# A hybrid decoder step on one core: reordered loads, a pipelined second split of x, half-width recurrence states, and convolution products on GpSimd

## Chip, cores and metric

The kernel runs on one core of a Trainium2 chip. The metric is the device time of one launch in microseconds. The core has five engines with their own instruction streams: TensorE (PE, matrix products; PEld is its weight load), VectorE (DVE), ScalarE (ACT), GpSimd (POOL) and SyncE (SP, which issues most DMAs).

## What is computed

One layer of a decoder over 1024 prompt positions and 8 x 8 sample positions (1088 columns together, width 1024), all in fp32:

```python
h = rmsnorm(x, norm_mix_pre)
(a_b, a_c, a_u, b_p, c_q, c_f, c_i, c_g, d_a, d_g) = split(h @ w_in, 10)   # 256 wide each
ya = a_b * causal_dwconv(a_c * a_u, conv_w)                  # width 3
yb = pool_scale * (W_grp @ (windowed means(b_p) - b_p))
f  = lb + (1 - lb) * sigmoid(c_f)                             # 4 heads of 64
S_t = diag(f_t) S_{t-1} + (1 - f_t) i_t^T ;  o_t = S_t^T silu(c_q)_t
yc = head_rmsnorm(o) * silu(c_g)
yd = silu(layernorm(causal_dwconv(d_a * sigmoid(d_g), conf_dw) + conf_b))   # width 31
x = x + rmsnorm(concat(ya, yb, yc, yd) @ w_out)
x = x + rmsnorm((silu(g @ w_gate) * (g @ w_up)) @ w_down),   g = rmsnorm(x)
```

The samples carry their own histories and states; all final states are outputs too.

## The kernel before

Activations lie transposed: 8 tiles of 128 features by 1088 columns (`ys[k]` holds x, then other results). Each fp32 product is three passes on TensorE: an operand is split into a rounded part and its remainder, both in a reduced format, `XH[k]` and `XL[k]` for x and two halves of a `wop` tile for the weights; the passes are hi by hi, hi by low, low by hi. A split is a copy on ACT (the rounded part) and a subtraction on DVE (the remainder).

`w_in` is taken in 20 units of 128 output columns, in the order `UNITS` (12, 10, 8, 18, 16, ...). The first four are called U0 to U3: U0 is half of the recurrence's input i, U1 of its gate f, U2 of its query q, U3 of the convolution module's gate. A unit has 8 steps, one for each k, of 9 products (three passes by the three column pieces `CH`). Weights arrive in raw tiles (`load_w`, `load_unit`, 4 buffers, one half unit each); `split_w`, `prep_half` and `prep_steps` split them. PSUM has 6 banks for units (`mm`, two units of three) and 2 for everything small (`sm`).

The start is a block written out by hand for ACT, DVE and PE:

1. For each k, raw x times the norm's gain is split into `XH`, `XL` (`split_x`), squared on ACT and added up on DVE (`acc0`), while PE multiplies U0 by it, and U1 three tiles later. So U0 to U2 work on x that has the gain but not yet the reciprocal root.
2. PE sums the squares over the partitions (line 266), DVE makes the reciprocal root `r0` in 12 short instructions, PE broadcasts it (line 189) and ACT copies it to `rb0`. U1 and U2 are multiplied by `rb0` when they leave PSUM (to `HF[0]` and `HQ[0]`, then sigmoid and silu).
3. The second split: for each k, x is scaled by gain and `rb0` (on DVE, `y<-y,prm,h` in the trace), copied to `XH[k]` (line 219) and subtracted to `XL[k]`. From U3 on, all units work on this x.

After the block, `drive` emits a unit's products and calls `hook` between them. `hook` has a budget of DVE time, counted up by the products and spent on the generators in the lists `first`, `crit` and `bulk`, in this order; each `yield` gives what the step costs, and `yield None` (`wait(n)`) says that the generator is not to be asked again in this hook. So the order of PE and DVE instructions is fixed when the program is built. The two hand-written blocks each keep their own order; the compiler's scheduler merges them, which is why the trace shows the recurrence's first DVE steps between those of the second split. `take` and `give` count buffers: `z` (two tiles), `h` (six), `sm`, `mm` and so on. `until` calls `hook` with no products between.

The generators that the change touches or its steps depend on:

- `hgrn(j)`: the recurrence for two of the four heads. Lines 700 and 702 make f and 1 - f on ACT; then DVE reciprocals and products for the first half of the columns, then products of the two heads (line 738, which wait for all of that), and so on by doubling block sizes. At the end it walks 9 groups of 128 columns: an update `up` (line 874), a transpose of k (853), the heads' outputs (878), the product with the state (890), and on DVE the new state in one of three tiles `sbd`. A state tile is 128 x 128 with two 64 x 64 blocks on its diagonal, one for each head, and zeros elsewhere.
- `d_conv(j)`: the convolution of width 31. For the samples it multiplies windows of u by the taps into a z tile (4 DVE instructions for half of the samples) and reduces it; for the prompt it does 31 DVE steps over 1024 columns. It is the main filler of `bulk`.
- `c_v`, `d_gate`, `d_val` and the other handlers take a unit out of PSUM; several need a z tile.

The mixers' outputs then go through `w_out`, and the second half of the layer runs the large feed-forward products, with Strassen-like combinations of blocks; the change does not touch it.

Of the kernel before, what the change touches and what calls it, by code (L numbers as in the profile page):

```python
# [52 lines left out]
def body(ctx, tc, xT, win, wout, wgu, wdn, par, con, msk, poolw, s_conv, s_pool, s_hgrn, s_conf,  # L53
# [31 lines left out]
    taps = T(mp, [P, 62], "taps")  # L85
    SY.dma_start(taps, par[:, NPAR:])
    cst = T(const, [P, NCON], "cst")
    SY.dma_start(cst, con)
    ident = cst[:, C_ID:C_ID + P]
# [103 lines left out]
    def load_unit(n):  # L193
        wraw[n] = [load_w(win[n][:, h * 4:h * 4 + 4]) for h in range(2)]
# [14 lines left out]

    for k in range(KT):  # L210
        if k in (0, 2):
            load_unit(U0 if k == 0 else U1)
        SY.dma_start(ys[k], xT[k * P:(k + 1) * P, :])
    load_unit(U2)

    def split_x(k, scale, parts):
# [23 lines left out]
    with tc.manual_schedule(engines={mybir.EngineType.Activation, mybir.EngineType.DVE, mybir.EngineType.PE}):  # L240
        sq, acc0 = {}, None
        pu[U0], pu[U1] = banks(), banks()
        prep_half(U0, 0)
        for k in range(KT):
            split_x(k, pc("g_mix", k), CH if k == 0 else [(0, NT)])
            if k == 0:
                prep_half(U0, 1)
            if k in (2, 3):
                prep_half(U1, k - 2)
            sq[k] = ht(NT)  # L250
            S.activation(sq[k], ys[k], AF.Square)
            mm_unit(U0, k)
            if k >= 3:
                mm_unit(U1, k - 3)
            if k == 1:
                acc0 = sq[0]
            if k >= 1:
                TT(acc0, acc0, sq[k], ALU.add)
        zv.append(zt())
        for c, (o, n) in enumerate(CH):  # L260
            S.copy(zv[0][:, o:o + n], pu[U0][c][:, :n])
        mm_unit(U1, 5)
        st = sm()
        V.memset(st[64:, 8:9], 1.0)
        for i, (go, gn) in enumerate(GRP):
            PE.matmul(st[:gn, i:i + 1], acc0[:, go:go + gn], ones[:, :1], start=True, stop=True, skip_group_check=True)
        mm_unit(U1, 6)
        for r0 in rsqrt_steps(st[:, :9], [P, 9], 1.0 / D, "x"):
            pass
        prep_half(U2, 0)  # L270
        prep_half(U2, 1)
        load_unit(U3)
        mm_unit(U1, 7)
        pu[U2] = banks()
        rb0 = ht(NT)
        for c, (o, n) in enumerate(CH):
            ps = sm()
            for i, (go, gn) in enumerate(GRP):
                if o <= go < o + n:
                    bcast(ps, r0[:, i:i + 1], gn, go - o)  # L280
            S.copy(rb0[:, o:o + n], ps[:, :n])
            mm_unit(U2, c)
        HF[0] = ht()
        for c, (o, n) in enumerate(CH):
            TT(HF[0][:, o:o + n], pu[U1][c][:, :n], rb0[:, o:o + n])
        S.activation(HF[0], HF[0], AF.Sigmoid)
        mm_unit(U2, *range(3, KT))
        prep_half(U3, 0)
        prep_half(U3, 1)
        for k in range(KT):  # L290
            STT(ys[k], ys[k], pc("g_mix", k), rb0, ALU.mult, ALU.mult)
            split_x(k, None, [(0, NT)])
            if k == 3:
                HQ[0] = ht()
                for c, (o, n) in enumerate(CH):
                    TT(HQ[0][:, o:o + n], pu[U2][c][:, :n], rb0[:, o:o + n])
                S.activation(HQ[0], HQ[0], AF.Silu)

# [119 lines left out]
    for t in qz:  # L418
        GP.memset(t, 0.0)
    sbd = [T(mp, [P, P], f"sbd{i}") for i in range(3)]  # L420
    for t in sbd:
        GP.memset(t, 0.0)

# [46 lines left out]
    def d_conv(j):  # L470
# [17 lines left out]
        for w in range(31):  # L488
# [206 lines left out]
    def hgrn(j):  # L695
# [172 lines left out]
        for g in range(9):  # L868
# [4 lines left out]
            if g < 8:  # L873
                PE.matmul(up, kt[:gn], v[:gn, g], start=True, stop=True, skip_group_check=True)
                k_token(g + 1, tp)
                pe(0.22)
# [12 lines left out]
            elif g > 0:  # L889
                PE.matmul(op[:, :gn], sbd[g % 3], q[:, go:go + gn], start=False, stop=True, skip_group_check=True)  # L890
                pe(0.22)
# [3 lines left out]
            if g < 8:  # L895
                nkt = k_evac(g + 1, tp)
                nx = sbd[(g + 1) % 3]
                for h, hs in enumerate(HEADS):
                    if g == 0:
                        V.tensor_copy(nx[hs, hs], up[hs, hs])  # L900
                    else:
                        STT(nx[hs, hs], sbd[g % 3][hs, hs], tots[128][hs, g:g + 1], up[hs, hs])
                give(sm=1)
                kt = nkt
                if g == 7:
                    for hs in HEADS:
                        SY.dma_start(o_hgrn_p[j][hs], nx[hs, hs])
                yield 0.4
            else:
# [976 lines left out]
```

## Time and profile before

| | us |
|---|---|
| median of 3 runs | 1186.87 (1184.63 to 1189.62) |
| the profiled execution | 1185.16, span 1182.8 |
| PE busy | 1145.1 (97%), granted clock 0.988 |
| PE weight loads | 1108.7 (94%) |
| DVE busy | 902.6 (76%) |
| ACT busy | 457.1 (39%) |
| POOL busy | 104.9 (9%) |

The span runs from the first to the last instruction; the 2.4 us around it belong to the launch. A timeline row reads: start, length, engine, line, operation, output from inputs by the program's names, shapes, count; in brackets the idle time ahead of it and who ended it. Several like instructions in a row are merged. A row of the chain of waits reads: start, length, engine, what. A row of the lines view reads: line, engine, operation, names, shapes and count, then busy time and mean ns, then idle time ahead of the group and who ended it. Line 65 is the helper for all `tensor_tensor`, 71 that for `scalar_tensor_tensor`.

### The profile page before, as it was taken

The numbers are of one execution on the slowest core, as the hardware profiler recorded it, in microseconds if no ns is written. First come the engines' busy times: TensorE is split into PE (matmuls) and PEld (weight loads), VectorE is DVE, ScalarE is ACT, GpSimd is POOL, SyncE is SP. The second block draws the span as 40 slices with busy tenths as digits, with TensorE's granted clock in tenths as the row PEclk, the third lists the DMA queues.
The fourth block names the chain that finished last, engine by engine and source line by source line (L and its number), as shares of the span: only waits on it lengthen the run. The fifth ranks groups of instructions, "written<-read, shape, count | busy, mean of one in ns | idle before, by whom it ended". The sixth has DMA issues, their size and how long they took to land.

```text
span 1182.8 us, 21814 instructions
## 1 busy us (share of the span) xinstructions
PE 1145.1 (97%) x8435; PEld 1108.7 (94%) x8435; DVE 902.6 (76%) x1827; ACT 457.1 (39%) x993; POOL 104.9 (9%) x170
## 2 busy tenths in 40 slices
PE   5979999999999999999999999999999999999995
PEld 4959989998899999999999999999999999999995
DVE  6498998997774678786766877787776658888666
ACT  7452431253264454343323443444444441223321
POOL 1000000000000000000000000000000232336323
PEclk9979999999999999999999999999999999999998
DMA  7101112211126114122331543553554787853555
GB/s 263 37 19 41 37 37 57 52 37 22 48 92 208 52 62 136 44 73 82 110 117 46 186 144 89 185 163 98 168 166 140 212 266 213 278 177 110 155 105 100
DMA packets 103319, 136.90 MB, mean 116 GB/s; under 512 B 25008, under 2 KB 72240, under 8 KB 103216
## 3 DMA queue, kind: packets, MB, share of 16 engines
q1 hardware_dynamic: 94864, 108.71, 29.5%
q0 software_dynamic: 8352, 26.81, 8.5%
q8 instruction: 66, 1.08, 0.4%
q14 instruction: 37, 0.30, 0.1%
HBM read 94.90 MB, written 40.57 MB: 115 GB/s over the span
## 4 chain that ended last, share of the span: by engine, by line
PE 88%; DVE 7%; ACT 2%; DMA 1%; issue 1%; SPq 0%; POOL 0%; DVEq 0%; ACTq 0%; POOLq 0%
PE p L1396 30%; PE mm L989 16%; PE p L1629 14%; PE p L1124 8%; PE p L1305 6%; PE p L1506 6%; PE mm L148 3%; PE sm L803 2%; DVE wop L65 1%; DVE y L71 1%; DVE xl L65 1%; DVE raw L65 1%; DMA raw<-wgu 1%; DMA y<-xT 1%; PE p L1090 1%
## 5 line engine op out<-in xcount | busy, mean ns | idle before, releaser
L65 DVE TENSOR_TENSOR wop<-raw,wop 128x512 fp32r<-128x512 f32 (+2 forms) x296 | 195.8, 675 | 98.1 <-ACT wop L1012 89.8
L1396 PE MATMUL p<-xh,wop 128*128 128x272 f32 x1216 | 235.6, 289 | 0.6 <-DVE c L65 0.6
L1012 ACT CAST wop<-raw 128x512 fp32r<-128x512 f32 (+1 forms) x240 | 141.9, 604 | 239.6 <-DVE raw L65 111.5
L1396 PEld LDWEIGHTS p<-xh,wop 128*128 128x128 f32 x1216 | 193.1, 188 | 0.8 <-DVE c L65 0.8
L989 PE MATMUL mm<-xh,wop 128*128 128x256 f32 (+2 forms) x816 | 172.8, 338 | 6.9 <-ACT xh L219 6.9
L1396 PE MATMUL p<-t,wop 128*128 128x272 f32 x912 | 177.2, 288 | 0.0
L1396 PE MATMUL p<-xl,wop 128*128 128x272 f32 x608 | 175.0, 288 | 0.0
L989 PEld LDWEIGHTS mm<-xh,wop 128*128 128x128 f32 x816 | 132.4, 192 | 15.1 <-ACT xh L219 9.5
L1396 PEld LDWEIGHTS p<-t,wop 128*128 128x128 f32 x912 | 144.7, 188 | 0.0
L1396 PE MATMUL p<-x,wop 128*128 128x272 f32 x456 | 130.5, 286 | 0.0
L1396 PEld LDWEIGHTS p<-xl,wop 128*128 128x128 f32 x608 | 114.6, 188 | 0.0
L1124 PE MATMUL p<-xh,wop 128*128 128x272 f32 x512 | 99.1, 290 | 0.0
L989 PE MATMUL mm<-xl,wop 128*128 128x256 f32 (+2 forms) x408 | 94.7, 341 | 1.3 <-DVE xl L65 1.0
L1396 PEld LDWEIGHTS p<-x,wop 128*128 128x128 f32 x456 | 85.8, 188 | 0.0
L1629 PE MATMUL p<-xh,wop 128*128 128x272 f32 x456 | 82.0, 288 | 0.2 <-DVE acc L65 0.2
L1629 PE MATMUL p<-xl,wop 128*128 128x272 f32 x456 | 81.4, 288 | 0.0
L1124 PEld LDWEIGHTS p<-xh,wop 128*128 128x128 f32 x512 | 81.0, 188 | 0.0
L65 DVE TENSOR_TENSOR raw<-raw,raw 128x512 f32<-128x512 f32 (+1 forms) x123 | 71.4, 591 | 9.7 <-DMA raw<-wgu 7.1
L71 DVE SCALAR_TENSOR_TENSOR y<-u,taps,y 128x1024 f32<-128x1024 f32 x60 | 77.0, 1283 | 1.5
L1124 PE MATMUL p<-xl,wop 128*128 128x272 f32 x256 | 73.9, 289 | 1.1 <-DVE xl L65 1.1
L1305 PE MATMUL p<-xh,wop 128*128 128x272 f32 x384 | 74.1, 290 | 0.0
L989 PEld LDWEIGHTS mm<-xl,wop 128*128 128x128 f32 x408 | 66.5, 192 | 7.4 <-DVE xl L65 3.9
(312 smaller groups left out, 2017.3 us busy)
## 6 DMA issues: line engine op xcount, KB each, us to landing
raw<-wgu SPq DMA_DIRECT2D x88, 256.0 KB, 3.3
hx<-hi SPq DMA_DIRECT2D x84, 136.0 KB, 2.4
raw<-win SPq DMA_DIRECT2D x40, 256.0 KB, 2.9
hx<-x SPq DMA_DIRECT2D x64, 136.0 KB, 2.7
raw<-wdn SPq DMA_DIRECT2D x32, 256.0 KB, 3.7
xh<-hx POOLq DMA_DIRECT2D x15, 544.0 KB, 5.3
xl<-hx POOLq DMA_DIRECT2D x15, 544.0 KB, 5.4
x<-hx POOLq DMA_DIRECT2D x12, 544.0 KB, 5.3
```

The costliest lines, as they stand in the source:

```text
L65: (eng or V).tensor_tensor(out, a, b, op)
L71: (eng or V).scalar_tensor_tensor(out=out, in0=a, scalar=s, in1=b, op0=op0, op1=op1)
L148: PE.matmul(ps[c][:, :n], hl[:, wi, kk], X[k][:, o:o + n], start=k == 0 and wi == 0 and X is XH, stop=k == KT - 1 and wi == 1)
L803: PE.matmul(ps[:rows, g * P:(g + 1) * P], kk[:, o:o + rows], qz[hf][:, :, g * 64:(g + 1) * 64], start=True, stop=True, skip_group_check=True)
L989: PE.matmul(ps[c][:, :w], hl[:, wi, kk], X[k][:, o:o + w], start=k == order[0] and wi == 0 and X is XH, stop=k == order[-1] and wi == 1)
L1012: S.copy(hl[:, 0], raw)
L1090: PE.matmul(st[:, i:i + 1], sq[:, a:a + P], ones[:, :1], start=first and i == 0, stop=last, skip_group_check=True)
L1124: PE.matmul(ps[nt][:, :PW], WO[nt][k // 4][:, wi, kk:kk + P], X[k][:, o:o + PW], start=k == korder[0] and wi == 0 and X is XH, stop=k == k ...
L1305: PE.matmul(ps[r][:, :PW], w[:, wi, (k % 4) * P:(k % 4 + 1) * P], X[k][:, o:o + PW], start=k == 0 and wi == 0 and X is XH, stop=k == KT - ...
L1396: PE.matmul(ps[:, :PW], wop[:, wi, kk * P:(kk + 1) * P], x(kk, xi), start=first and kk == 0 and wi == 0 and xi == 0, stop=kk == 3 and wi == 1,
L1506: PE.matmul(ps[:, :n], wd[:, wi, kk * P:(kk + 1) * P], hops[k][xi][:, o:o + n], start=first and kk == 0 and wi == 0 and xi == 0, stop=not ...
L1629: PE.matmul(ps[:, :PW], ws[name][wi][q], x[:, xi, pr], start=first and q == 0 and wi == 0 and xi == 0, stop=q == 1 and wi == 1, skip_group ...
```

## The change

Four edits:

- **Loads.** U0's and U1's halves are spread between the x tiles, x tile 0 comes in two pieces, the constants `cst` after x tile 3 and the convolution's `taps` last.
- **The start.** In step 1 a tile's square and sum come one tile later (`square(k - 1)` after the split of k), and U0's second and U1's halves are split at other places. The sums over the partitions come one step of U1 earlier, and two of U1's steps move behind them. In step 3 the subtraction for tile k - 1 comes after the scaling of tile k; `HF[0]` and `HQ[0]` leave PSUM at other places, and both sigmoid and silu come behind the last copy to `XH`.
- **States.** `sbd` is 128 x 64, one head above the other, with no zeros. Update and state product are done head by head on TensorE; the new state is one DVE instruction instead of two.
- **Sample products.** The 16 window products of `d_conv` run on GpSimd, and five waits stand ahead of the reduction.

```diff
-    SY.dma_start(taps, par[:, NPAR:])
-    SY.dma_start(cst, con)
...
-    for k in range(KT):
-        if k in (0, 2):
-            load_unit(U0 if k == 0 else U1)
-        SY.dma_start(ys[k], xT[k * P:(k + 1) * P, :])
+    load_half(U0, 0)
+    load_x(0, CH[0], (CH[1][0], NT - CH[1][0]))
+    load_x(1)
+    load_half(U0, 1)
+    load_x(2)
+    load_half(U1, 0)
+    load_x(3)
+    SY.dma_start(cst, con)
+    load_x(4)
+    load_half(U1, 1)
+    for k in range(5, KT):
+        load_x(k)
     load_unit(U2)
+    SY.dma_start(taps, par[:, NPAR:])
...
         for k in range(KT):
             split_x(k, pc("g_mix", k), CH if k == 0 else [(0, NT)])
-            if k == 0:
+            if k == 1:
                 prep_half(U0, 1)
-            if k in (2, 3):
-                prep_half(U1, k - 2)
-            sq[k] = ht(NT)
-            S.activation(sq[k], ys[k], AF.Square)
+            if k in (2, 5):
+                prep_half(U1, k // 5)
+            if k >= 1:
+                square(k - 1)
             mm_unit(U0, k)
             if k >= 3:
                 mm_unit(U1, k - 3)
-            if k == 1:
-                acc0 = sq[0]
-            if k >= 1:
-                TT(acc0, acc0, sq[k], ALU.add)
+        square(KT - 1)
...
-        mm_unit(U1, 5)
         st = sm()
...
-        mm_unit(U1, 6)
+        mm_unit(U1, 5)
...
-        mm_unit(U1, 7)
+        mm_unit(U1, 6)
...
-            mm_unit(U2, c)
-        HF[0] = ht()
...
-        S.activation(HF[0], HF[0], AF.Sigmoid)
-        mm_unit(U2, *range(3, KT))
-        prep_half(U3, 0)
-        prep_half(U3, 1)
-        for k in range(KT):
-            STT(ys[k], ys[k], pc("g_mix", k), rb0, ALU.mult, ALU.mult)
-            split_x(k, None, [(0, NT)])
-            if k == 3:
-                HQ[0] = ht()
...
+            if c == 0:
+                mm_unit(U1, 7)
+            else:
+                mm_unit(U2, c - 1)
+        mm_unit(U2, *range(2, KT))
...
+        for k in range(KT):
+            scale_x(k)
+            if k >= 1:
+                low_x(k - 1)
+            if k == 2:
+                HF[0] = evac_r(U1)
+            if k == 4:
+                prep_half(U3, 0)
+                prep_half(U3, 1)
         S.activation(HF[0], HF[0], AF.Sigmoid)
+        low_x(KT - 1)
+        HQ[0] = evac_r(U2)
+        S.activation(HQ[0], HQ[0], AF.Silu)
...
-    sbd = [T(mp, [P, P], f"sbd{i}") for i in range(3)]
-    for t in sbd:
-        GP.memset(t, 0.0)
+    sbd = [T(mp, [P, 64], f"sbd{i}") for i in range(3)]
...
-                TT(t[:, b * 8:(b + 1) * 8], win_ap, dwb[:, 0])
+                TT(t[:, b * 8:(b + 1) * 8], win_ap, dwb[:, 0], eng=GP)
+            yield from wait(5)
...
-            yield 2.6
+            yield 1.4
...
-                PE.matmul(up, kt[:gn], v[:gn, g], start=True, stop=True, skip_group_check=True)
+                for hs in HEADS:
+                    PE.matmul(up[hs, :64], kt[:gn, hs], v[:gn, g, hs], start=True, stop=True, skip_group_check=True)
...
-                PE.matmul(op[:, :gn], sbd[g % 3], q[:, go:go + gn], start=False, stop=True, skip_group_check=True)
+                for hs in HEADS:
+                    PE.matmul(op[hs, :gn], sbd[g % 3][hs], q[hs, go:go + gn], start=False, stop=True,
+                              skip_group_check=True)
...
-                for h, hs in enumerate(HEADS):
-                    if g == 0:
-                        V.tensor_copy(nx[hs, hs], up[hs, hs])
-                    else:
-                        STT(nx[hs, hs], sbd[g % 3][hs, hs], tots[128][hs, g:g + 1], up[hs, hs])
+                if g == 0:
+                    V.tensor_copy(nx, up[:, :64])
+                else:
+                    STT(nx, sbd[g % 3], tots[128][:, g:g + 1], up[:, :64])
```

In the new second split, `scale_x` is the scaling and the copy to `XH`, `low_x` the subtraction, `evac_r` the three products with `rb0` out of PSUM.

More of the change, by code (lines that the diff above doesn't have):

```diff
@@ L206, in body, with load_half, load_x @@
     U0, U1, U2, U3 = UNITS[:4]
-    for k in range(KT):
-        if k in (0, 2):
-            load_unit(U0 if k == 0 else U1)
-        SY.dma_start(ys[k], xT[k * P:(k + 1) * P, :])
+    def load_half(n, h):
+        wraw.setdefault(n, []).append(load_w(win[n][:, h * 4:h * 4 + 4]))
+    def load_x(k, *cols):
+        for o, n in cols or [(0, NT)]:
+            SY.dma_start(ys[k][:, o:o + n], xT[k * P:(k + 1) * P, o:o + n])
+    load_half(U0, 0)
[10 more added lines that the diff above has]
+        load_x(k)
     load_unit(U2)
+    SY.dma_start(taps, par[:, NPAR:])
     def split_x(k, scale, parts):
@@ L240, in body, with square @@
     with tc.manual_schedule(engines={mybir.EngineType.Activation, mybir.EngineType.DVE, mybir.EngineType.PE}):
-        sq, acc0 = {}, None
+        sq = {}
         pu[U0], pu[U1] = banks(), banks()
+        def square(k):
+            sq[k] = ht(NT)
+            S.activation(sq[k], ys[k], AF.Square)
+            if k:
+                TT(sq[0], sq[0], sq[k], ALU.add)
         prep_half(U0, 0)
@@ L265, in body @@
         for i, (go, gn) in enumerate(GRP):
-            PE.matmul(st[:gn, i:i + 1], acc0[:, go:go + gn], ones[:, :1], start=True, stop=True, skip_group_check=True)
-        mm_unit(U1, 6)
+            PE.matmul(st[:gn, i:i + 1], sq[0][:, go:go + gn], ones[:, :1], start=True, stop=True, skip_group_check=True)
+        mm_unit(U1, 5)
         for r0 in rsqrt_steps(st[:, :9], [P, 9], 1.0 / D, "x"):
@@ L281, in body, with scale_x, low_x, evac_r @@
             S.copy(rb0[:, o:o + n], ps[:, :n])
-            mm_unit(U2, c)
-        HF[0] = ht()
-        for c, (o, n) in enumerate(CH):
-            TT(HF[0][:, o:o + n], pu[U1][c][:, :n], rb0[:, o:o + n])
-        S.activation(HF[0], HF[0], AF.Sigmoid)
-        mm_unit(U2, *range(3, KT))
-        prep_half(U3, 0)
-        prep_half(U3, 1)
-        for k in range(KT):
-            STT(ys[k], ys[k], pc("g_mix", k), rb0, ALU.mult, ALU.mult)
-            split_x(k, None, [(0, NT)])
-            if k == 3:
-                HQ[0] = ht()
-                for c, (o, n) in enumerate(CH):
-                    TT(HQ[0][:, o:o + n], pu[U2][c][:, :n], rb0[:, o:o + n])
-                S.activation(HQ[0], HQ[0], AF.Silu)
+            if c == 0:
[3 more added lines that the diff above has]
+        mm_unit(U2, *range(2, KT))
+        def scale_x(k):
+            STT(ys[k], ys[k], pc("g_mix", k), rb0, ALU.mult, ALU.mult)
+            S.copy(XH[k], ys[k])
+        def low_x(k):
+            TT(XL[k], ys[k], f32(XH[k]), ALU.subtract)
+        def evac_r(n):
+            t = ht()
+            for c, (o, w) in enumerate(CH):
+                TT(t[:, o:o + w], pu[n][c][:, :w], rb0[:, o:o + w])
+            return t
+        for k in range(KT):
[7 more added lines that the diff above has]
+                prep_half(U3, 1)
+        S.activation(HF[0], HF[0], AF.Sigmoid)
+        low_x(KT - 1)
+        HQ[0] = evac_r(U2)
+        S.activation(HQ[0], HQ[0], AF.Silu)
     MM = 0.1135
@@ L905, in hgrn @@
                 if g == 7:
-                    for hs in HEADS:
-                        SY.dma_start(o_hgrn_p[j][hs], nx[hs, hs])
-                yield 0.4
+                    SY.dma_start(o_hgrn_p[j], nx)
+                yield 0.25
             else:
```

## The prediction

> **What bounds the kernel now.** I read the windows first, cut where the work changes character: the loads, the first products on raw x, the second split of x, the rest of the mixers, everything after. Columns are: stretch, length, then busy time of PE, its weight loads, DVE, ACT, POOL, then granted TensorE clock, DMA share and GB/s.
>
> ```profile
> 0.00:10.00 10.00, 0.00 (x0) 0.00 (x0) 2.06 (x9) 2.33 (x4) 3.75 (x12) 1.00 0.67 206
> 10.00:66.00 56.00, 49.41 (x282) 44.02 (x282) 37.00 (x48) 36.11 (x50) 0.00 (x0) 0.99 0.35 122
> 66.00:87.00 21.00, 15.76 (x57) 11.59 (x57) 20.53 (x29) 8.59 (x8) 0.00 (x0) 0.62 0.07 25
> 87.00:347.00 260.00, 259.21 (x1703) 237.16 (x1701) 226.71 (x376) 97.26 (x232) 0.98 (x6) 1.00 0.16 41
> 347.00:1182.80 835.80, 820.68 (x6396) 815.96 (x6396) 616.31 (x1368) 312.80 (x701) 100.16 (x152) 0.99 0.46 140
> ```
>
> From 87 to 347 us PE is busy 259.2 of 260 us: there only PE time counts, and DVE time is free as long as DVE keeps up. Room lies only ahead of 87 us: 10 us with no matmul, and 66 to 87 us, where PE did 57 matmuls at a granted clock of 0.62 while DVE was busy 20.5 of 21 us. After 347 us nothing is edited, so it is only shifted. So the question is when PE gets through the front, and what the edits add to PE after it.
>
> The chain of waits and the timeline of the front:
>
> ```profile
> 3.07 6.62 DMA y<-xT
> 9.78 1.57 ACT L222 ACTIVATE xh<-y,prm 128x256 fp32r<-128x256 f32 x3 [3.46 <-DMA y<-xT]
> 12.78 1.18 ACT L222 ACTIVATE xh<-y,prm 128x1088 fp32r<-128x1088 f32 x1
> 17.73 0.69 DVE L65 TENSOR_TENSOR wop<-raw,wop 128x512 fp32r<-128x512 f32 x1
> 18.33 1.29 DVE L65 TENSOR_TENSOR h<-h,h 128x1088 f32<-128x1088 f32 x1
> 19.53 1.35 DVE L71 SCALAR_TENSOR_TENSOR xl<-y,prm,xh 128x1088 fp32r<-128x1088 f32 x1
> 20.93 16.45 PE mm L148 x98
> 37.39 1.88 PE sm L266 x18
> 46.50 0.53 ACT L281 COPY h<-sm 128x448 f32<-128x448 f32 x1 [1.52 <-PE sm L189]
> GB/s 0 22 69 207 272 221 271 322 313 363 410 422 427 418 422 418 409 407 394 312 272 68 106 321 191 110 347 222 29 0 16 0 0 0 8 0 0 0 0 0
> ```
>
> (The last row is the GB/s of each us of the first 40.) x tile 0 lands at 9.69, its split starts at 9.78, and PE runs without a gap only from 20.93, when the low part of tile 3 (19.53 + 1.35) is there. From then on PE is the bound: 11 steps (one unit, one k: 9 matmuls) in 16.45 us, 1.5 us a step, then the sums of squares, until the broadcast reciprocal root rb0 is complete at 47.03. That is the start of the second split.
>
> **The change, part by part.**
>
> *Loads.* Before x tile 0 on SP's queue stood 25+31+87+512 KB; it landed when the GB/s row sums to 1.95 MB, though only 1.2 MB of the queue ends with it: later transfers overtake by 0.75 MB. After the edit prm, half a unit, x0 and x1 are 1.37 MB; with the same 0.75 MB that is 2.12 MB, or 10.1 us in the row, less 0.9 us for two small issues (taps, cst) that leave the head: x1 at 9.2 us. From there the new order runs xh1, the second weight half, a square, xh2, the next half, a square on ACT (1.18 for a split; a square of the same tile about as much, a cast of 512 columns half, estimates from that row), which ends near 14.8, and on DVE a weight half, one addition and xl3 (0.6 + 1.2 + 1.2 by starts, 1.35 with its end), which end at 17.6 us, against 20.9. I take a gain of 3.3. Bounds: 1.5 if the overtaking doubles, 4.9 if x lands in its queue place and ACT and DVE alone set the pace. PE then has no new gap: a tile needs 2.5 us on DVE (1.35 + 1.29, overlapped) and gives PE 3.0 us of work. cst is read first by the broadcasts, taps by the convolution after the second split: both have over 15 us of work as cover. U2's loads still wait on SP for a free buffer, with taps now behind them; a late taps would cost only from there on.
>
> *Sums one step earlier.* The statistics now come ahead of U1's step 5: 1.5 us less before them, and the two steps after them still hide the root. rb0 is complete at 47.0 - 3.3 - 1.5 = 42.2 us.
>
> *Second split.* Its rows, and the recurrence's first half that follows (HF, HQ are h tiles):
>
> ```profile
> 47.05 1.28 ACT L286 ACT_TABLE_LOAD   x1
> 48.34 1.11 ACT L286 ACTIVATE h<-h 128x1088 f32<-128x1088 f32 x1
> 50.39 1.30 ACT L700 ACTIVATE h<-h,low,oml 128x1088 f32<-128x1088 f32 x1
> 57.45 1.29 DVE L65 TENSOR_TENSOR xl<-y,xh 128x1088 fp32r<-128x1088 f32 x1 [1.17 <-ACT xh L219]
> 58.66 1.34 DVE L71 SCALAR_TENSOR_TENSOR y<-y,prm,h 128x1088 f32<-128x1088 f32 x1
> 64.76 1.20 ACT L702 ACTIVATE h<-h,ones 128x1088 f32<-128x1088 f32 x1
> 66.10 1.41 DVE L65 TENSOR_TENSOR h<-mm,h 128x256 f32<-128x256 f32 x3
> 67.42 1.34 DVE L71 SCALAR_TENSOR_TENSOR y<-y,prm,h 128x1088 f32<-128x1088 f32 x1
> 68.69 0.72 DVE L68 TENSOR_SCALAR h<-h 128x1088 f32<-128x1088 f32 x1
> 69.32 1.29 DVE L65 TENSOR_TENSOR wop<-raw,wop 128x512 fp32r<-128x512 f32 x2
> 72.51 1.29 DVE L65 TENSOR_TENSOR xl<-y,xh 128x1088 fp32r<-128x1088 f32 x1 [0.24 <-ACT xh L219]
> 80.61 0.42 DVE L71 SCALAR_TENSOR_TENSOR h<-h,h 128x128 f32<-128x128 f32 x1
> 81.52 2.08 PE L738 MATMUL sm<-h 64*128 64x128 f32 x16
> ```
>
> Before, each tile pays y 1.27, an ACT wait of 1.17 and xl 1.21; from tile 4 on, the recurrence's DVE work fills those waits. PE cannot pass L738 (it stands inside U3's step 6) until that work ends at 80.9. After, the wait is gone, but the same rows show what is late next: the sigmoid of HF, hidden at 48.34 now, moves behind the last xh, so L700, L702 and all of the recurrence come after the whole split. From rb0: y0 to y7 8 x 1.27, xl0 to xl5 6 x 1.21, HF's evacuation 1.32 (66.10 to 67.42), U3's weight halves 1.2 and 0.6 of wait for their casts: y7 ends after 20.4. Then xh7 1.15, table and sigmoid 2.4, L700 1.2, L702 1.2, and the recurrence's half: from 68.69 to 80.9, without two y, two xl and 0.24 of wait inside it, 7.0. Sum 33.4: L738 at 75.6 us instead of 81.5, a gain of 5.9 (of which 1.1 is the pipeline's own). If ACT takes the Silu of HQ with its table ahead of L702, 2.4 is lost: 78.0, a gain of 3.5. I take the first, as the Silu waits for an evacuation that ends 1.3 after xl7, later than the sigmoid. PE sits idle about 11 us ahead of L738 and starts slow, as it does now (2.08 for 16 there, 1.16 in the quoted row below): nothing gained, nothing lost. Bounds with the loads': 1.7 and 7.5.
>
> *States as 64 columns.* Timeline of one group step, of the small products with half-sized operands, and two groups of the lines view:
>
> ```profile
> 146.64 0.65 PE L989 MATMUL mm<-xh,wop 128*128 128x256 f32 x3
> 147.13 0.38 PE L874 MATMUL sm<-vtok,khat 128*128 128x128 f32 x2
> 147.35 0.27 PE L853 MATMUL sm<-cst,h 128*128 128x128 f32 x1
> 147.55 0.44 PE L878 MATMUL sm<-attn,vtok 128*64 128x128 f32 x4
> 147.92 0.49 PE L890 MATMUL sm<-h,sbd 128*128 128x128 f32 x2
> 148.16 0.74 PE L989 MATMUL mm<-xh,wop 128*128 128x256 f32 x3
> 92.81 1.15 PE L989 MATMUL mm<-xh,wop 128*128 128x256 f32 x6
> 93.89 1.16 PE L738 MATMUL sm<-h 64*128 64x128 f32 x16
> 299.36 0.33 PE L878 MATMUL sm<-attn,vtok 64*64 64x64 f32 x4
> 299.62 0.83 PE L883 MATMUL sm<-h,s 128*128 128x8 f32 x6
> L71 DVE SCALAR_TENSOR_TENSOR sbd<-sbd,tot,sm 64x64 f32<-64x64 f32 x28 | 7.8, 279 | 8.1 <-ACT khat L859 7.3
> L65 DVE TENSOR_TENSOR z<-u,taps 128x248 f32<-128x248 f32 x16 | 5.6, 412 | 0.0
> ```
>
> By starts, the update costs 0.22 (147.13 to 147.35) and the state's output 0.24 (147.92 to 148.16), two instructions each. After, each is four: the update about 0.26 (299.36 to 299.62, four of 64x64), the output 4 x 0.07 = 0.27 (1.16 over 16). Besides, PE changes between full and half operands more often. Such a change shows as 0.1: six products take 1.08 ahead of L738 against two steps of 0.49, and one transpose ahead of L878 takes 0.20 where its pair rate is 0.11. The update brings two more per group (into it, and back for the transpose). That is 16 updates x 0.24 and 14 outputs x 0.03, +4.3 us, in a stretch where PE is the bound. Lower bound 1.1 (no change costs), upper 8.8 (every instruction at L878's 0.09, and a change at the output too). The middle is nearest to these rows. On DVE 28 updates become 14: 4 us saved on an engine that is not the bound.
>
> The Trainium skill, TensorEngine Tiling (Array Packing), Key Properties, says that a change of tiling mode drains TensorE, and that different tiles can load and multiply in parallel. By the first sentence the price stays at 4.3; by the second alone the four instructions would take half their time and the part would cost nothing.
>
> *Convolution products on POOL.* 16 DVE instructions (5.6 us) leave, no PE instruction changes. POOL has nothing else to do there (0.98 us in 260). The reduction now waits for four POOL products; five waits in the order are five parts of a unit step (0.5 or 1.0 us each), some 4 us of PE work, between. Gain or loss: DVE idles 33 us in those 260, so up to 9.6 us saved buy nothing, and a late reduction costs nothing unless DVE becomes the bound: 0.
>
> The Trainium skill, GPSIMD Engine Reference, Key points, speaks against this part: POOL shares its SBUF interfaces with DVE when DVE has two SBUF inputs. It would lengthen the convolution's DVE instructions; no row of this stretch shows it.
>
> *Sum.* -5.9 + 4.3 = -1.6 us on the profiled execution's 1185.16 (span 1182.8 and 2.4 around it), 1183.6; that execution lies 1.7 under the median, so 1185.3 on its scale. With the Silu first it is 1187.7. Both are no change: 0.5% is 5.9 us, about what a measurement of this kernel can tell from none (its three runs lie 5 us apart).
>
> **The rivals.**
>
> 1. *Faster: the halves overlap and x lands in its queue place.* For it: L738's 0.07 per instruction is less than L878's 0.09, although its weights are twice as wide, so two row halves overlap somewhat. Against: L878's two heads show no overlap. Gain 7.5, price 1.1: -6.4, 1180.5. Chance 0.27. The Tiling page's parallel tiles are this mechanism.
> 2. *Slower: a z tile held.* The convolution now keeps one of two z tiles over five waits, twice per channel half; its steps run only when the recurrence lets them. A unit's gate or value then waits for z, its three banks stay full, and the order goes on with DVE work but no products. DVE is then ahead of PE in the order, and PE waits at the next small product. It decides from 7.5 us of such waiting; the worst is one whole unit, 8 x 1.5 = 12 us: 1197. Against: a unit has 12 us before its banks are missed, and the products of one hold are 1.4 us on DVE (5.6 over four). Chance 0.08.
> 3. *Slower: the group steps at 8.8 us, Silu first, loads gaining 1.5.* -1.7 + 8.8 = +7.1: 1194. Chance 0.08.
> 4. *The pipeline is none.* If copies of v, which need U3's transposes, sit between the xh on ACT, DVE waits 1.17 per tile again: +8, 1193. Chance 0.04.
>
> **How the numbers follow.** The forecast, with either order of Silu and L702, has 0.53: 1185.3, its own range 1182 to 1190. Leaving out 0.1 at each end, the range is 1180 to 1193.5. Faster by over 0.5% 0.27 (rival 1), within 0.53, slower 0.20 (rivals 2 to 4).
>
> **What would show it.** First gapless PE work near 17.6 us; rb0 complete near 42; DVE without waits from then to the last xl; HF's sigmoid after it, PE idle some 11 us, and L738 near 75.6 (78 if the Silu is first). The group step from update to next unit product 1.03 us now, about 1.3 after; DVE's idle time between 87 and 347 us larger by some 10 us with PE still full. It is wrong if PE's idle time ahead of L738 is filled, if L738 stands elsewhere in the order, if the group steps stay at 1.03, or if PE shows gaps behind units whose z is held.

## The result and the profile after

| | before | after |
|---|---|---|
| median, us | 1187.93 (1184.63 to 1189.62, 4 runs) | 1199.95 (1198.89 to 1202.27, 4 runs) |
| profiled execution, us | 1185.16, span 1182.8 | 1199.3, span 1197.5 |

The changed kernel is slower: ratio 1.0107, 95% interval 1.0079 to 1.0136. The forecast was no change, 1185.3 us, with an upper end of 1193.5. A few executions at a granted clock of 0.56 to 0.70 (one each of before, e13 and e16, 1522 to 1879 us) are left out of all times below.

The same windows as in the prediction (stretch, length, busy time of PE, weight loads, DVE, ACT, POOL, then granted clock, DMA share, GB/s), and the windows of PE alone where the mixers end and the output product begins:

```profile
10.00:66.00 56.00, 51.38 (x291) 48.09 (x292) 43.72 (x52) 33.75 (x48) 0.00 (x0) 0.97 0.33 116
66.00:87.00 21.00, 8.30 (x45) 7.54 (x44) 13.92 (x24) 9.08 (x10) 0.00 (x0) 0.67 0.08 26
87.00:347.00 260.00, 259.16 (x1727) 230.94 (x1726) 206.24 (x325) 87.53 (x214) 15.27 (x22) 1.00 0.16 40
...
340.00:350.00 10.00, 7.76 (x54) 1.00 0.09 26
350.00:360.00 10.00, 4.39 (x15) 0.60 0.09 26
360.00:370.00 10.00, 9.54 (x53) 0.71 0.50 151
```

From 87 to 347 us PE is as full as it was, and DVE does 20 us less. The loss stands behind that: between 340 and 370 us PE is idle for 8.3 us, and then runs at 0.60 and 0.71 of its clock. The same 30 us before, as one window, and the product after which its PE had no gap:

```profile
340.00:370.00 30.00, 28.94 (x226) 1.00 0.66 215
...
347.74 0.39 PE L1124 MATMUL p<-xl,wop 128*128 128x272 f32 x1 [1.06 <-DVE xl L65]
```

Timeline of the changed kernel's PE at that place:

```profile
350.83 0.62 PE L187 MATMUL sm<-cst,rs_lny 128*128 128x128 f32 x4 [2.48 <-DVE y L65]
355.04 0.60 PE L1157 MATMUL p<-xh,wop 128*128 128x272 f32 x1 [3.59 <-ACT xh L1068]
363.58 0.60 PE L1157 MATMUL p<-xl,wop 128*128 128x272 f32 x1 [0.15 <-DVE xl L65]
```

PE waits for the layer norm behind the wide convolution (`rs_lny` is its reciprocal root, y its result) and then for the splits of its result. Single products take 0.60 us there. The Trainium skill, TensorE: Matmul & The Clock Gate, Part 1, has the array's clock fall to half after about one idle window of 3.4 us; the gaps and the clock of 0.60 here agree with it.

Taken apart from one fixed point to the next: the first attention product starts 1.0 us earlier (80.50 for 81.52); from there to the end of the last unit product it takes 267.1 us for 262.7, +4.4 (347.6 - 80.5 against 344.2 - 81.5); from there to the first gapless output product 15.9 us for 3.6, +12.4. Behind it some 1 us comes back. That makes the 14.7 us by which the two spans differ. The tail, from the last unit product to the gapless output product, is the surprise.

Where the convolution went, in the timeline of the changed kernel (line 65 on POOL are the four products of a half, line 516 the reduction, line 68 the first of the 31 prompt steps, y<-sm,y the layer norm):

```profile
103.85 3.55 POOL L65 TENSOR_TENSOR z<-u,taps 128x248 f32<-128x248 f32 x4 [100.03 <-DVE u L65]
117.21 1.18 DVE L516 TENSOR_REDUCE cr<-z 128x32 f32<-128x992 f32 x1
118.47 4.02 POOL L65 TENSOR_TENSOR z<-u,taps 128x248 f32<-128x248 f32 x4 [11.07 <-DVE cr L516]
133.20 1.18 DVE L516 TENSOR_REDUCE cr<-z 128x32 f32<-128x992 f32 x1
134.57 0.81 DVE L68 TENSOR_SCALAR y<-u,taps,prm 128x1024 f32<-128x1024 f32 x1
249.91 0.81 DVE L68 TENSOR_SCALAR y<-u,taps,prm 128x1024 f32<-128x1024 f32 x1
326.38 0.76 DVE L71 SCALAR_TENSOR_TENSOR y<-sm,y 128x256 f32<-128x256 f32 x2 [1.17 <-PE sm L539]
...
103.00:135.00 32.00, 19.19 (x34) 1.00 0.16 38
```

POOL is done at 107.4, but the reduction comes at 117.2; from products to reduction it is 13.4, 14.7 and, for the second pair, 22 and 21 us. Its row names no wait: it was put there by the order. In the 32 us of the last row DVE, which has the convolution as its filler, works for only 19.2 us. The 31 steps of the second pair begin at 249.9.

### The profile page after: what moved, and what is told of

It reads as the page before. It is cut to its first block, busy times and chain, and to the rows that moved or that the text cites. A ratio compares the mean times of both kernels' runs of the same rounds, so it can differ in the third digit from the quotient of the medians.

```text
span 1197.5 us, 21915 instructions
## 1 busy us (share of the span) xinstructions
PE 1152.7 (96%) x8495; PEld 1112.0 (93%) x8495; DVE 897.3 (75%) x1795; ACT 457.2 (38%) x993; POOL 119.1 (10%) x183
## 4 chain that ended last, share of the span: by engine, by line
PE 88%; DVE 3%; ACT 1%; issue 0%; POOL 0%; POOLq 0%; DVEq 0%; ACTq 0%
PE p L1429 33%; PE mm L1022 16%; PE p L1662 14%; PE p L1157 8%; PE p L1539 6%; PE p L1338 6%; PE sm L835 1%; DVE xl L65 1%; PE sm L911 1%; PE p L1123 0%; PE sm L924 0%; ACT xh L1068 0%; PE sm L885 0%; PE sm L770 0%; PE sm L907 0%
## 5 line engine op out<-in xcount | busy, mean ns | idle before, releaser
L65 DVE TENSOR_TENSOR wop<-raw,wop 128x512 fp32r<-128x512 f32 (+2 forms) x296 | 198.8, 685 | 95.1 <-ACT wop L1045 90.4
L1022 PE MATMUL mm<-xh,wop 128*128 128x256 f32 (+2 forms) x816 | 168.9, 334 | 3.2 <-ACT wop L139 3.2
L65 DVE TENSOR_TENSOR t<-p,t 128x272 f32<-128x272 f32 (+3 forms) x138 | 60.6, 449 | 16.5 <-PE p L1662 8.7
```

The costliest lines, as they stand in the source:

```text
L65: (eng or V).tensor_tensor(out, a, b, op)
L1022: PE.matmul(ps[c][:, :w], hl[:, wi, kk], X[k][:, o:o + w], start=k == order[0] and wi == 0 and X is XH, stop=k == order[-1] and wi == 1)
```

## The experiments

Two theories stood at the outset. W: the five waits hold the convolution back. P: work on GpSimd costs by itself. A third came up on the way. C: the cost that `d_conv` reports for a half, changed from 2.6 to 1.4 us in the same edit. Durations of the stretches are from one profiled execution each, times are medians; before was run again beside each group and lay between 1186.9 and 1187.9 us. "Loss" below is what PE lost in a profile: idle time plus (1 - clock) x busy time, summed over 10 us windows, first from 90 to 340 us (the mixers), then from 340 to 380 us (the tail). The profiled execution is not always near the median: e12's took 1202.93 us and e13's 1215.62, some 5 us more, e17's 1190.86 and e10's 1193.44, 2 to 3 us less.

| run | products on | waits | cost | us | ratio (interval) | loss, mixers | loss, tail |
|---|---|---|---|---|---|---|---|
| before | DVE | 0 | 2.6 | 1187 | | 0.5 | 1.1 |
| after | POOL | 5 | 1.4 | 1199.95 | 1.0107 (1.0079-1.0136) | 0.2 | 12.8 |
| e1 | DVE | 0 | 2.6 | 1186.89 | 0.9997 (0.9981-1.0012) | 3.8 | 1.1 |
| e2 | POOL | 0 | 1.4 | 1203.36 | 1.0141 (1.0113-1.0170) | 18.9 | 1.1 |
| e3 | DVE | 5 | 1.4 | 1200.06 | 1.0115 (1.0081-1.0148) | 0.6 | 12.3 |
| e10 | DVE | 2 | 1.4 | 1195.51 | 1.0071 (1.0054-1.0087) | 3.2 | 5.0 |
| e12 | DVE | 0 | 1.4 | 1198.25 | 1.0108 (1.0090-1.0125) | 15.9 | 1.1 |
| e17 | DVE | 0 | 2.0 | 1193.54 | 1.0055 (1.0036-1.0073) | 6.3 | 1.1 |
| e14 | DVE | 5 | 2.6 | 1210.08 | 1.0198 (1.0179-1.0216) | 0.0 | 22.5 |
| e13 | POOL | 5 | 2.6 | 1209.82 | 1.0206 (1.0183-1.0229) | 3.7 | 21.8 |
| e16 | POOL | 0 | 2.6 | 1186.34 | 0.9995 (0.9981-1.0008) | 3.8 | 1.1 |

All but the first row have the other three edits. With engine, five waits or none, and cost 1.4 or 2.6, all eight combinations are there. 3.4 us of the mixers' loss in e1, e13, e16 and e17 are a low clock on a PE that is busy (last section).

**e1: the convolution's edit undone** (products, waits and cost as before).

> The kernel after, with the convolution's sample products back on DVE and no waits (loads, start and half-width states stay). Theory W (the five waits hold back the convolution's 31 prompt steps, so the layer norm behind them ends late and the last stretch before the output projection runs dry): the 13 us between the end of the last unit and gapless projection go, 1187 us, first prompt step of the first channel half near 112 us instead of 134.6. Theory P (the products on GpSimd themselves cost, by a shared port or by their length): 1187 too. Theory S (the half-width state products are the loss): still 1200.

Back at par: all of the 13 us hang on this edit. In its profile the convolution is where it was before, and DVE is full in the stretch that was 19 us:

```profile
104.17 1.19 DVE L515 TENSOR_REDUCE cr<-z 128x32 f32<-128x992 f32 x1
110.75 0.80 DVE L68 TENSOR_SCALAR y<-u,taps,prm 128x1024 f32<-128x1024 f32 x1
285.42 0.76 DVE L71 SCALAR_TENSOR_TENSOR y<-sm,y 128x256 f32<-128x256 f32 x2
...
103.00:135.00 32.00, 30.27 (x47) 1.00 0.16 45
```

**e2: products on GpSimd, the waits taken out.** **e3: waits kept, products on VectorE.**

```diff
 e2:              TT(..., eng=GP)
-            yield from wait(5)
 e3:
-                TT(..., eng=GP)
+                TT(...)
             yield from wait(5)
```

> The kernel after, products on GpSimd, only the line with the five waits taken out, so the reduction stands right behind the products in the order. Theory W: DVE waits up to 4 us for GpSimd four times, at places where it has slack, prompt steps start early: 1187 to 1191 us. Theory P: 1198 or more. Theory S: 1200.

> The kernel after with the five waits kept, but the sample products on DVE: GpSimd has no part. Theory W: 1199 to 1201 us, with the first prompt steps near 134 and 250 us as in the kernel after. Theory P: 1187. Theory S: 1200, with the prompt steps anywhere.

e3 said W: without GpSimd the same time, the same holds (first prompt steps at 133.84 and 248.80 us), the same tail. But e2 has no waits and lost even more, as P had it. Its profile shows both sides: DVE waits 5.1 us for GpSimd's products, and PE 3.9 us at one place for DVE's mask copies; its loss lies in the mixers, not in the tail. So there were two ways to lose, and neither theory had both.

**e5: instead of the waits, four prompt steps between products and reduction. e9: the same with the products on VectorE; e15 is e9 once more (its name promises a cost of 2.6 us that it doesn't have).**

```diff
-            yield from wait(5)
+            for _ in range(4):
+                tap(w)
+                w += 1
+                yield 1.2
...
-        for w in range(31):
...
+        for w in range(w, 31):
+            tap(w)
```

> The changed kernel with the products still on GpSimd, but the five waits between products and reduction replaced by four prompt steps of VectorE for each half (the same steps, only earlier). Theory W (the waits hold the convolution back, GpSimd itself costs nothing): no hold is left and the four steps, 4 x 1.2 = 4.8 us, cover the 2.6 to 5.2 us that GpSimd's four products took; as the kernel with the convolution undone, 1187 us (1185 to 1190), the first project product near 350 us, VectorE waiting for GpSimd under 1 us in all. Theory P (work handed to GpSimd costs by itself, by VectorE instructions that grow longer beside it or by the hand-over): 1192 us or more, and VectorE's steps beside the products longer than 1.25 us each.

> As the kernel with four prompt steps between products and reduction, but with the products on VectorE again. In that kernel VectorE's instructions beside GpSimd's products were longer by about 0.5 us each (0.92 for 0.42 us, 0.79 for 0.29 us, 0.77 for 0.24 us), 3.2 us between 193 and 208 us, and TensorE then waited 3.23 us for a mask copy of VectorE. Theory G (GpSimd's products cost by lengthening VectorE's instructions beside them): without them 1187 us (1185 to 1190), no TensorE wait of over 1 us between 90 and 290 us. Rival (the moved steps push the mask copies back in VectorE's order, wherever the products run): 1196 us or more, with the wait of some 3 us still there near 215 us.

> The kernel with four prompt steps between products and reduction, products on VectorE, run once more unchanged beside the others of this group, at a reported cost of 1.4 us: 1200 us (1197 to 1203) by either theory.

1200.70, 1200.35 and 1199.74 us: GpSimd has no part in it, though my row for it was real. Nor do these runs show that a filled hold costs: their tail loses 1.1 us, as without waits, and the mixers lose 11.6, 11.4 and 11.0. In e9 PE waits 3.0 us for the mask copies (at 216.5) and 1.6 us for DVE's `s`; e12 below has the same two waits, 3.2 and 1.6 us, with no step moved. What they share with it is the reported cost of 1.4; the moved steps with 2.6 were not run. Timeline of DVE in e5, beside GpSimd's products and after them:

```profile
193.60 0.92 DVE L71 SCALAR_TENSOR_TENSOR h<-h,h 128x144 f32<-128x144 f32 x1
195.61 0.42 DVE L65 TENSOR_TENSOR h<-h,h 128x144 f32<-128x144 f32 x1
205.47 1.78 DVE L65 TENSOR_TENSOR wop<-raw,wop 128x512 fp32r<-128x512 f32 x2
```

The first ran beside the products and took 0.5 us more than it does alone (0.42 in e1), the pair of weight halves 1.78 for 1.28. The Trainium skill, GPSIMD Engine Reference, Key points, names shared SBUF interfaces for this; these rows agree. But theory G, which made that the cause, fell with e9.

**e10: two waits instead of five, products on VectorE. e11: the kernel before with the convolution's edit alone.**

> The changed kernel with the products on VectorE and two waits instead of five. Theory W (each wait holds the convolution for one more time that the recurrence asks for filler, and the end moves by what the chain convolution, layer norm, project product is late): hold of 5 to 9 us instead of 13 to 23 us; if the loss goes with the number of waits, 1187 + 2/5 x 13 = 1192 us (1190 to 1195); the first project product near 350 + 2/5 x 5 = 352 us and the reductions of layer 0 near 110 and 120 us. Rival (a threshold: the chain behind the convolution has slack, and only a long hold uses it up): 1187 us, as without waits.

> The kernel before with only the convolution's part of the change (products on GpSimd, five waits, the later steps' costs as changed). If the loss sits in this part alone and does not need the new front: 1187 + 13 = 1200 us, the first project product 5 us later or more and single products waiting for the low half behind it. If it needs the new front or the states to lose time: 1187 us.

e10's tail loses 5.0 us, the share of two waits in e3's 12.3; its time is 8 us longer, not 5, but at par it is not, as a threshold would have had it. The edits are `wait(2)` for `wait(5)`, and the three lines of the convolution on the kernel before. e11 loses 15.6 us, 1203.29 (ratio 1.0132, 1.0116 to 1.0148), and again in the tail (17.5 us there, 1.3 in the mixers): first prompt steps at 135.75 and 251.46 us, PE waiting 4.8 us for `rs_lny`. The edit needs none of the others.

**e12 to e14, e16, e17: the reported cost.** Every kernel that had lost so far had the 1.4, and those at par had the 2.6.

```diff
 (no waits, products on VectorE)
-            yield 2.6
+            yield 1.4
```

> The changed kernel with the sample products on VectorE and no waits, as before the change, but with the changed cost that the filler reports for each half: 1.4 us in place of 2.6 us. Every kernel of this study that lost time by the convolution (waits with GpSimd, waits on VectorE, GpSimd without waits, steps in between) had the 1.4, and the one that lost nothing had the 2.6. Theory C (the reported cost: 1.2 us for each half that VectorE works and the plan does not count, so VectorE falls behind the plan and its mask copies and low halves come late): 1195 us or more. Theory W (the waits and the order): 1187 us (1185 to 1190), as with 2.6.

> The changed kernel, GpSimd and five waits kept, with the cost of each half reported as 2.6 us again. Theory C: 1187 to 1190 us. Theory W: 1200 us (1197 to 1203), reductions near 117, 133, 225 and 248 us as before this edit.

> Products on VectorE, five waits, and the cost reported as 2.6 us: against the first kernel of this group the waits are the only thing that can differ from the kernel with the convolution undone. Theory C: 1187 us. Theory W: 1200 us (1197 to 1203).

e12 is the plainest run of the study: one number in the planning of the order, no instruction more or less, +11 us. `hook` spends a budget of DVE time on fillers; a half that reports 1.4 us and keeps DVE for 1.40 + 1.19 + 0.24 = 2.83 us lets it emit 2.4 us too much for a pair of halves, compared with 2.6. DVE then lags behind the order, and TensorE's small products come before their inputs. The attention products, their mask copies on DVE and the next attention product, in e1 and then in e12:

```profile
209.35 1.16 PE L769 MATMUL sm<-h 64*128 64x128 f32 x16
213.19 1.36 DVE L774 COPY_PREDICATED attn<-mk,sm 128x512 f32<-128x512 uint32 x2
215.09 0.33 PE L782 MATMUL sm<-h 64*64 64x64 f32 x4
```

```profile
211.13 1.16 PE L769 MATMUL sm<-h 64*128 64x128 f32 x16
217.89 1.32 DVE L774 COPY_PREDICATED attn<-mk,sm 128x512 f32<-128x512 uint32 x2
218.66 0.33 PE L782 MATMUL sm<-h 64*64 64x64 f32 x2 [3.21 <-DVE attn L774]
...
200.00:220.00 20.00, 16.52 (x111) 0.99 0.18 53
300.00:340.00 40.00, 38.38 (x214) 0.79 0.13 23
```

3.8 us from products to copies became 6.8, and PE waited 3.2. In e1 the same two stretches hold 20.00 us of PE work at 1.00, and 40.00 at 0.91. So not all of the low clock in the second goes with the waits: both profiles have some 10 us near 0.66 (310 to 320 us in e12, 315 to 325 in e1) with no wait ahead. In e12 PE then waits 1.62 us for DVE's `s` at 325.6, and has 0.54 and 0.72 from 325 to 330 and to 340, where e1 has 1.00.

But the cost isn't the whole cause: with 2.6 restored the waits lose not 13 but 23 us, on either engine (e13, e14). e14's windows of PE and its timeline:

```profile
340.00:370.00 30.00, 15.23 (x56) 0.61 0.23 71
...
346.75 4.00 PE L427 MATMUL sm<-ones,h 128*128 128x1 f32 x18 [4.18 <-DVE h L65]
362.26 0.59 PE L1157 MATMUL p<-xh,wop 128*128 128x272 f32 x1 [4.58 <-ACT xh L1068]
```

So the two parts of the edit work against each other in the changed kernel: the waits push the convolution late and leave the tail idle, the low cost draws it early and leaves DVE behind in the mixers. With the waits, going from 2.6 to 1.4 moves the second pair's first prompt step from 261.4 (e14) to 248.8 us (e3) and takes the tail's loss from 22.5 to 12.3. Waits alone are +23 us, the cost alone +11, both +13; the waits lose in the tail, the cost in the mixers. Theory C, as I put it for e13 and e14 (1187), fell; what holds is that each of the two is enough.

e16 is e2 with `yield 2.6`, e17 is e12 with `yield 2.0`.

> The changed kernel with the products on GpSimd, without the five waits, and with the cost of each half reported as 2.6 us. Theory C (without waits, the loss comes from reporting less than VectorE is then busy or held: with 1.4 us VectorE's mask copies came 6.8 us instead of 3.8 us behind their products and TensorE waited 3.2 us for them; the 2.6 us also cover VectorE's waits for GpSimd, 0.6 to 2.5 us each): 1187 to 1191 us, and no TensorE wait of over 1.5 us on the mask copies between 90 and 290 us. Rival (GpSimd's products cost by themselves when VectorE waits for them): 1198 us or more.

> Products on VectorE, no waits, the cost of each half reported as 2.0 us, between the two run so far (2.6 us: 1187 us; 1.4 us: 1198 us). If the loss goes with the unreported time: 1192 to 1193 us. If it is a threshold (the lag of VectorE either fits into TensorE's queue of filler or it doesn't): within 2 us of one of the two.

e16 is at par: GpSimd's products cost nothing once the waits are out and the order counts the DVE time rightly. Its reductions show why 2.6 is right there, although DVE no longer multiplies:

```profile
106.97 1.19 DVE L515 TENSOR_REDUCE cr<-z 128x32 f32<-128x992 f32 x1 [2.48 <-POOL z L65]
109.51 1.19 DVE L515 TENSOR_REDUCE cr<-z 128x32 f32<-128x992 f32 x1 [0.63 <-POOL z L65]
203.02 1.19 DVE L515 TENSOR_REDUCE cr<-z 128x32 f32<-128x992 f32 x1 [1.94 <-POOL z L65]
```

DVE stands 5.0 us for POOL over four halves, 1.3 for each, and 1.43 + 1.3 is again some 2.7 us for which DVE is not to be had. That is what e2 left uncounted (+16 us). But e12 leaves as much uncounted, 2.83 - 1.4, and loses 11: with the low cost GpSimd's products were some 5 us dearer (1203.36 against 1198.25, the intervals of the ratios just overlap), and what these 5 us are stays open. e17, at 2.0 us, loses 6 us, about the middle of 0 and 11: by this one point between, it goes with the unreported time, not by a threshold.

**e4, e6 to e8, e18: the other edits, and what is left in them.** e4 is the kernel before with the new loads and start; e6 has the 64-column states alone.

> The kernel before with the new loads and the new start alone (full-width states, sample products on DVE, no waits). From the two traces the front gains 1.0 us at the recurrence's first products, and the group steps cost PE about 4 us: Theory W with that price: 1183 to 1186, 4 us under the kernel with only the convolution undone. If the half-width states cost nothing: 1187, the same as that kernel.

> The kernel before with the recurrence's states as 64 columns, nothing else. By the predicted size (+4.3 us over 65 group steps, four half-height products in place of two): 1191.5 us, ratio 1.0036. By the difference of the two runs that share the front (with and without 64 columns: 353.36 - 79.41 = 273.95 us and 351.49 - 82.56 = 268.93 us from the first attention product to the gapless project products): +5.0 us, 1192 us. By their medians alone (1186.89 against 1184.99): +1.9 us, 1189 us. If the states cost nothing: 1187 us.

e4: 1184.99 us, ratio 0.9976 (0.9956 to 0.9996), some 2 us gained. e6: 1188.40, ratio 1.0007 (0.9995 to 1.0019). Its first attention product stands at 80.86 and the gapless output product at 351.50, 270.6 us, against 81.52 and 347.74, 266.2, with the loss in the mixers alike (0.4 and 0.5): +4.4 us. The two spans differ by 2.4 (0.7 less ahead of that stretch, 1.4 less behind it), the medians by 1.4, which the interval does not tell from nothing; the 1191.5 us that the predicted size would have given did not come. (The group steps are 16 updates and 14 outputs, not the 65 of the expectation.)

```diff
 e7:         for k in range(KT):
                 scale_x(k)
+                if k == 3:
+                    S.activation(HF[0], HF[0], AF.Sigmoid)
 ...
-        S.activation(HF[0], HF[0], AF.Sigmoid)
 ...
-        S.activation(HQ[0], HQ[0], AF.Silu)        # e7 and e8: now in hgrn(0), behind the second gate
```

> The kernel before with the new loads and the new start, and in it the forget gate's sigmoid issued beside the fourth scaling step, as early as its input allows, and the query's Silu issued behind the two gate activations of the recurrence instead of ahead of them. Theory S (the first attention product waits for the chain of ACT behind the last split: table load, sigmoid, gate, table load, Silu, second gate): the two gate activations start at about 67 us, VectorE's clamp ends near 70 us, the first attention product near 76 to 78 us instead of 82.56, and as the units behind it follow without gaps the end moves by as much: 1179 to 1181 us, ratio 0.993 to 0.995 against the kernel before. Rival (the start of the recurrence does not count, its fillers do): first attention product as early, but 1185 us as with the front alone. Rival (the sigmoid delays the splits in the pipeline by a table load of 1.28 us and 1.11 us): last low half later by up to 2.4 us, 1183 us.

> As the run before it, but only the Silu is moved behind the two gate activations; the sigmoid stays behind the last split. Theory S: the clamp is freed of a table load and of the Silu, 1.28 + 1.11 us; first attention product 2.4 us earlier than with the front alone, near 79 to 80 us, 1182.5 us. If the start does not count: 1185 us.

e7: 1182.86, ratio 0.9951 (0.9933 to 0.9969), faster than both kernels. e8: 1186.0, ratio 0.9980 (0.9966 to 0.9994); in its trace the Silu still ran ahead of the second gate (at 70.26 and 71.28 us), since the compiler's scheduler put it there, so it is e4 again and didn't test its theory. The chain in e7:

```profile
63.36 1.13 ACT L307 CAST xh<-y 128x1088 fp32r<-128x1088 f32 x1
65.16 1.20 ACT L735 ACTIVATE h<-h,ones 128x1088 f32<-128x1088 f32 x1
66.38 1.28 ACT L737 ACT_TABLE_LOAD   x1
67.06 0.72 DVE L68 TENSOR_SCALAR h<-h 128x1088 f32<-128x1088 f32 x1
74.21 2.08 PE L773 MATMUL sm<-h 64*128 64x128 f32 x16 [6.20 <-DVE h L71]
```

From the last copy to `XH` to the attention product it takes 10.85 us; in the changed kernel 15.55 (64.95 to 80.50), in e4 15.54 and in e8 15.56. The product came earlier than theory S had it (76 to 78), and yet the time stayed above its 1179 to 1181: of the 4.7 us some 2 to 3 arrive in it (1182.86 against e4's 1184.99 and e8's 1186.0).

> The kernel with the new loads, the new start and the two gates first (1182.9 us), with the cost of each half reported as 3.2 us instead of 2.6 us; VectorE's own work for a half is 1.40 + 1.19 + 0.24 = 2.83 us. If the loss went on with the reported cost beyond what VectorE does (9.5 us for each us, from 1198 at 1.4 and 1187 at 2.6): 1177 us. Theory C (only the unreported part costs, and at 2.6 it is 0.2 us for each half, with no TensorE wait on the mask copies left to remove): 1183 us (1181 to 1185). If a cost reported too high starves TensorE or delays the layer norm, as the waits did: 1186 us or more.

e18 is e7 with `yield 3.2`: 1181.09, ratio 0.9945 (0.9925 to 0.9964). That is not to be told from e7: beyond 2.6 us, near the 2.83 that DVE really works, no gain and no loss by the reported cost is seen. e7 and e18 are the fastest kernels of the study; what they gain is order, not work.

## Why the prediction was wrong

*The step that failed* is "Convolution products on POOL ... 0". It has two parts. "Five waits in the order are five parts of a unit step, some 4 us of PE work": the holds were 13 to 22 us from products to reduction, because a `wait` returns `None`, and the generator is then asked again only in the next hook that has budget left over from the recurrence; a filler of the lowest rank gets few of these. What budget a hook cannot spend is dropped (`min(state["budget"], 0.0)`), so the order doesn't make up the DVE time. "A late reduction costs nothing unless DVE becomes the bound": I asked whether DVE would be short of time, and it had time. But the 31 steps behind the reduction are the main filler of those gaps, and the layer norm and the last splits stand behind them: the norm came at 326.4 us in place of 288.3, and its end was no longer covered by unit products. And the line `yield 1.4` in the diff I didn't price at all. By e12, alone, it is +11 us. Without this edit the kernel, e1, is at 1186.9 us, well inside the range; but that is partly luck, as the front gained 1.0 us and not 3.5 or 5.9 and the group steps took their 4.4. The norm before:

```profile
288.28 0.76 DVE L71 SCALAR_TENSOR_TENSOR y<-sm,y 128x256 f32<-128x256 f32 x2
```

*Rival 2* named the waits and 1197 us, at a chance of 0.08; the place was right, the mechanism not. No unit was held by a z tile: PE is full from 87 to 347 us. What it said against itself, cover of 12 us in the banks, had nothing to do with what became late.

*Loads.* The first product came 4.8 us earlier (5.54 for 10.34) and the low part of tile 3 ended at 17.3 us, predicted 17.6: right. *Sums.* rb0 was complete at 43.5, not 42.2 (the last copy is the row at 42.99); the granted clock from 30 to 40 us was 0.83, at which 1.7 us of PE work are lost, and PE is the bound there. In before's profile it was 1.00.

*Second split.* The pipeline did what it should, but the Silu went first, the case I had put second, and xh7 came late behind copies of v and a weight cast:

```profile
42.99 0.53 ACT L298 COPY h<-sm 128x448 f32<-128x448 f32 x1 [1.54 <-PE sm L187]
64.42 0.62 ACT L139 CAST wop<-raw 128x512 fp32r<-128x512 f32 x1 [0.66 <-ACT vtok L716]
64.95 1.10 ACT L307 CAST xh<-y 128x1088 fp32r<-128x1088 f32 x1
66.07 1.28 ACT L327 ACT_TABLE_LOAD   x1
67.36 1.11 ACT L327 ACTIVATE h<-h 128x1088 f32<-128x1088 f32 x1
69.82 1.28 ACT L330 ACT_TABLE_LOAD   x1
72.13 1.19 ACT L734 ACTIVATE h<-h,ones 128x1088 f32<-128x1088 f32 x1
73.35 0.73 DVE L68 TENSOR_SCALAR h<-h 128x1088 f32<-128x1088 f32 x1 [4.64 <-ACT h L734]
80.50 2.08 PE L770 MATMUL sm<-h 64*128 64x128 f32 x16 [12.70 <-DVE h L71]
```

The clamp (line 68) needs the second gate, and that stands behind two table loads and two activations: DVE waits 4.64 us and PE 12.70. I argued that the Silu's input would be later than the sigmoid's end; but line 734 comes behind the Silu in ACT's order, so waiting longer for it would only have made it worse. Gain 1.0 us instead of 5.9: 1.3 of the 4.9 us are rb0's, 1.0 the late xh7 and 2.3 the Silu with its table load. Other profiles with the same start put this product anywhere from 78.2 (e14) to 82.9 us (e13). The sigmoid's move, which the prediction had named as "what is late next", was undone in e7, and the Silu put last: 4.7 us of the chain go. How they divide between the two is not shown, as e8 did not test the Silu alone.

*States.* Predicted +4.3 us on PE, from a mode change of 0.1 and four half products for two; in e6 +4.4 from the first attention product to the gapless output product, and in the changed kernel +4.4 to the end of the unit products. That the price is made up as predicted, of changes and products, no run shows. The group step in its timeline:

```profile
140.71 0.34 PE L907 MATMUL sm<-vtok,khat 128*64 128x64 f32 x4
140.98 0.33 PE L885 MATMUL sm<-cst,h 128*128 128x128 f32 x1
141.24 0.44 PE L911 MATMUL sm<-attn,vtok 128*64 128x128 f32 x4
141.61 0.43 PE L924 MATMUL sm<-h,sbd 64*64 64x128 f32 x4
141.97 0.77 PE L1022 MATMUL mm<-xh,wop 128*128 128x256 f32 x3
```

1.26 us from update to next unit product, predicted about 1.3, before 1.03.

## What to carry to other kernels

Where a program fixes the order of its engines by a plan with reported costs, a reported cost and a wait are part of the schedule like any instruction: price both, and ask of a filler that is held what stands behind its last step, not only whether its engine has time. Work that is moved off an engine must be reported with the time for which the first engine still stands waiting for it. And two faults that move the same work in opposite directions, one later and one earlier, can hide part of each other: undo the parts of an edit one by one, the numbers in it too, before naming one as the cause.

## What the runs showed of the hardware

DVE instructions beside GpSimd's two-input products took some 0.5 us longer in e5 (0.92 for 0.42, and 1.78 for 1.28 for a pair). In the changed kernel GpSimd's products took 0.9 to 1.2 us each in three of four halves (3.55 to 4.61 for four), and 0.66 in the other (2.63 for four). In three of four pairs of kernels this cost no time that can be seen (e13 against e14, after against e3, e16 against e1); in the fourth, e2 against e12, some 5 us.

The granted clock also falls without long gaps of PE. Between 290 and 340 us the profiles of e1, e4, e7, e8, e13, e16 and e17 lose 3.4 us each, after at most 0.5 us of idle time; those of before, e6, e3, e14 and the changed kernel lose none there. Between 30 and 40 us ten of the 17 profiles with the new start lose another 1.7 with no idle time there (0.69 from 35 to 40 us in the changed kernel's, 1.00 in e14's), and e11, with the old start, 1.7 between 30 and 50. These cuts are as large as what the edits of the start are worth, and they may be why runs of one kernel lie 5 us apart. What sets them off was not tried.
